# A decoder trunk's second feed-forward layer: two of four column slices of the down projection by seven block products

## The chip, the cores and the metric

The kernel runs on one core of a Trainium2 chip. The metric is the device time of one execution in microseconds (us); of several executions the median counts. Engines are named as in the profile: PE is TensorE (matmuls), PEld its weight loads, DVE is VectorE, ACT is ScalarE, POOL is GpSimd, SP is SyncE, which here only starts the transfers of weights.

## The reference

Two residual layers run over 256 tokens of width 2048, all in float32. The first mixes tokens with a convolution module, the second with a state-space module and a gated linear unit. Each is followed by a dense feed-forward layer of width 8192:

```python
def mlp(h, w_up, w_down):
    a = jax.nn.relu(h @ w_up)
    return (a * a) @ w_down
...
        h = rms_norm(x, mlp_norm[i])
        x = x + mlp(h, mlp_w_up[i], mlp_w_down[i])
    return rms_norm(x, final_norm)
```

The change concerns the feed-forward layer of i = 1, which is the last big stage. Its two weight matrices hold 2048 x 8192 float32 values each, 64 MB apiece, and every value is read from memory once per execution.

## The kernel before

**Splitting.** A float32 product is made from three matmuls of a type that keeps fewer bits: each operand is split into `hi` (a rounded copy) and `lo` (the rest), and hi*hi, hi*lo and lo*hi are summed in PSUM. For the weights, `split` (line 110) makes both parts for one half of a loaded piece: ACT writes `hi` (line 118), DVE writes `lo` = raw - hi (line 125), 128 x 1024 values each. There are four `hi` and four `lo` buffers, so a half can be split only when PE is done with the half four places earlier.

**Steps.** The weights come in steps of 1 MB (`raw`, three buffers), each of two halves. `run_steps` walks over the halves in order: it starts the loads of up to three steps beyond the current one, issues the splits up to three halves beyond the current one, and then the matmuls of the current half (`consume`). So the order in which steps are appended to `self.steps` is the order of PE's work. The framework then orders the instructions of each engine by priority; splits carry a raised one.

**The feed-forward layer** (`mlp`) cuts the width 8192 into eight slices of 1024. `up(s)` appends eight steps: four column groups of 256 (q), each with two halves of the contraction (kc). One half of such a step is eight matmuls with 512 columns (line 199: weights `hi` against both parts of the activations) and eight with 256 (line 202: `lo`). After every second step `relu2` turns the accumulator into squared, scaled and split activations `rT`. `down(s)` appends eight more: four output column slices of 512 (n), each with two halves of the contraction. Here the activations are the stationary operand; one half is twelve matmuls of 512 columns (lines 222 to 224), for two blocks of contraction, two token blocks of 128 and three products. After each n the sum in PSUM is added to `x` (`add_x`, line 820, 128 x 1024). The order is up(0), then up(s), down(s-1) for s = 1 to 7, then down(7). One pass of up(s) and down(s-1), from here on a slice, has 16 steps or 32 halves, 16 of up and 16 of down.

**Queues.** SP issues all weight loads (line 92) in step order; a load waits for its buffer, that is for the last `lo` made from it. DVE executes in the order written: `lo`, the activations' sums, and `add_x`.

## Time and profile before

| what | value |
|---|---|
| median of 3 runs | 1987.49 us (1987.08 to 1987.63) |
| span of the profiled execution | 1985.8 us |
| PE busy, share of the span | 1966.9 us, 99% |
| DVE busy | 1401.3 us, 71% |
| ACT busy | 952.4 us, 48% |
| last feed-forward stage, 1290 to 1970 us: PE busy of 680 us | 680.00 us |
| the same stage: DVE, ACT busy | 405.08 us, 317.93 us |
| the same stage: busy share of the DMA engines | 0.60 |

The profiled execution spans 1985.8 us from its first to its last instruction, and the median of the timed runs lies 1.7 us above that. In the rows below, a time in the first column of a timeline is the start in us from the beginning of the span. In a table by windows, each engine is given with its busy us in that window and, in brackets, its instructions. In a group of instructions, `x32 | 33.9, 1061` means 32 instructions, 33.9 us busy in all, 1061 ns for one; behind the second bar stands the idle time of the engine ahead of them and what ended it. Matmuls overlap in the pipeline: one lasts 0.39 us by the profile, but the next starts sooner, so PE's pace is read from the distance of starts.

### The profile page before, as it was taken

The page shows a single profiled execution, that of the slowest core. Times are in us where ns is not written, and L with a number is a line of the kernel's source. Part 1 is how long each engine was busy: PE and PEld are TensorE (multiplying, and loading weights), DVE is VectorE, ACT ScalarE, POOL GpSimd, SP SyncE. Part 2 cuts the span into 40 slices and gives each one's busy share as a digit, 9 for nine tenths or more (in the row PEclk, how much of TensorE's full clock was granted, in tenths as well). Part 3 has the DMA queues.
Part 4 walks back from the last instruction along what each step waited for, and adds up shares of the span by engine and source line. Part 5 has one row for each costly group of instructions (what it writes and reads, how often), then busy time and mean ns, then how long its engine had stood idle before and what let it go on. Part 6 is the DMA issues. An engine that isn't in the chain of part 4 may idle for free.

```text
span 1985.8 us, 28885 instructions
## 1 busy us (share of the span) xinstructions
PE 1966.9 (99%) x11604; PEld 1687.0 (85%) x11604; DVE 1401.3 (71%) x1904; ACT 952.4 (48%) x1179; POOL 274.8 (14%) x252
## 2 busy tenths in 40 slices
PE   8999999999999999999999999999999999999998
PEld 8999788888888888888888788888888888888887
DVE  6899798888787777777558847565555565555655
ACT  6443655544444544444445445454444454444444
POOL 3998300000000221222010000000000000000000
PEclk9999999999999999999999999999999999999999
DMA  8767458667686877877898865665666656565653
GB/s 228 190 184 207 147 183 267 206 226 245 200 260 192 214 229 253 265 246 238 319 308 298 304 215 186 191 191 189 193 190 192 190 191 191 190 213 190 192 191 128
DMA packets 317030, 428.49 MB, mean 216 GB/s; under 512 B 9761, under 2 KB 211553, under 8 KB 313537
## 3 DMA queue, kind: packets, MB, share of 16 engines
q1 hardware_dynamic: 300976, 384.59, 61.6%
q0 software_dynamic: 12352, 37.49, 6.3%
q10 hardware_dynamic: 3568, 4.56, 0.8%
q8 instruction: 91, 1.49, 0.3%
q14 instruction: 43, 0.35, 0.1%
HBM read 400.08 MB, written 34.91 MB: 219 GB/s over the span
## 4 chain that ended last, share of the span: by engine, by line
PE 96%; DVE 2%; DMA 1%; issue 0%; SPq 0%; POOL 0%; ACT 0%; POOLq 0%; DVEq 0%; ACTq 0%
PE acc L199 24%; PE acc L222 15%; PE acc L223 15%; PE acc L224 15%; PE acc L202 12%; PE acc L213 3%; PE acc L212 3%; PE acc L211 3%; PE pk L484 1%; DMA Vt<-Vd 0%; SPq L92 0%; PE kp L1113 0%; PE xw L1254 0%; DMA raw<-in_conv_w_in_dram 0%; PE xt L254 0%
## 5 line engine op out<-in xcount | busy, mean ns | idle before, releaser
L118 ACT ACTIVATE hi<-raw 128x1024 fp32r<-128x1024 f32 x672 | 711.6, 1060 | 953.5 <-PE acc L224 510.2
L125 DVE TENSOR_TENSOR lo<-raw,hi 128x1024 fp32r<-128x1024 f32 x611 | 747.9, 1226 | 505.6 <-ACT hi L118 501.3
L199 PE MATMUL acc<-hT,hi 128*128 128x512 f32 x2048 | 514.4, 393 | 0.0
L199 PEld LDWEIGHTS acc<-hT,hi 128*128 128x128 f32 x2048 | 368.9, 189 | 68.0 <-issue 1.6
L222 PE MATMUL acc<-hi,rT 128*128 128x512 f32 x992 | 387.2, 391 | 0.0
L223 PE MATMUL acc<-lo,rT 128*128 128x512 f32 x992 | 386.4, 390 | 0.0
L224 PE MATMUL acc<-hi,rT 128*128 128x512 f32 x992 | 386.0, 389 | 0.0
L202 PEld LDWEIGHTS acc<-hT,lo 128*128 128x128 f32 x2048 | 279.6, 190 | 20.0
L202 PE MATMUL acc<-hT,lo 128*128 128x256 f32 x2048 | 286.3, 282 | 0.0
L222 PEld LDWEIGHTS acc<-hi,rT 128*128 128x128 f32 x992 | 186.3, 188 | 39.6 <-issue 1.6
L224 PEld LDWEIGHTS acc<-hi,rT 128*128 128x128 f32 x992 | 186.3, 188 | 39.1
L223 PEld LDWEIGHTS acc<-lo,rT 128*128 128x128 f32 x992 | 186.3, 188 | 38.0 <-issue 0.2
L125 POOL TENSOR_TENSOR lo<-raw,hi 128x1024 fp32r<-128x1024 f32 x60 | 143.1, 2402 | 31.3 <-ACT hi L118 24.8
L211 PE MATMUL acc<-hT,hi 128*128 128x256 f32 x512 | 146.1, 286 | 0.9 <-ACT hi L118 0.9
L212 PE MATMUL acc<-hT,hi 128*128 128x256 f32 x512 | 145.7, 286 | 0.3 <-DVE hT L259 0.3
L213 PE MATMUL acc<-hT,lo 128*128 128x256 f32 x512 | 145.5, 286 | 0.0
L829 DVE SCALAR_TENSOR_TENSOR cv<-vT,dw,cv 128x256 f32<-128x256 f32 x348 | 141.3, 486 | 2.2 <-ACT cv L527 1.7
L820 DVE TENSOR_TENSOR x<-x,acc 128x1024 f32<-128x1024 f32 (+1 forms) x72 | 83.6, 1161 | 27.6 <-PE acc L224 22.0
L211 PEld LDWEIGHTS acc<-hT,hi 128*128 128x128 f32 x512 | 98.9, 193 | 3.0 <-issue 1.6
L222 PE MATMUL acc<-hi,yT 128*128 128x512 f32 x256 | 101.1, 395 | 0.0
L212 PEld LDWEIGHTS acc<-hT,hi 128*128 128x128 f32 x512 | 98.8, 193 | 2.2 <-issue 1.6
L223 PE MATMUL acc<-lo,yT 128*128 128x512 f32 x256 | 99.9, 390 | 0.6 <-DVE lo L125 0.6
(285 smaller groups left out, 1722.9 us busy)
## 6 DMA issues: line engine op xcount, KB each, us to landing
raw<-in_mlp_w_up_dram SPq DMA_DIRECT2D x128, 1024.0 KB, 5.8
raw<-in_mlp_w_down_dram SPq DMA_DIRECT2D x128, 1024.0 KB, 5.2
raw<-in_ssm_w_glu_dram SPq DMA_DIRECT2D x32, 1024.0 KB, 5.5
raw<-in_conv_w_in_dram SPq DMA_DIRECT2D x60, 512.0 KB, 5.6
raw<-in_conv_w_out_dram SPq DMA_DIRECT2D x16, 1024.0 KB, 5.2
Vd<-bv POOLq DMA_DIRECT2D x16, 512.0 KB, 6.3
Md<-Kd POOLq DMA_DIRECT2D x32, 256.0 KB, 7.2
Wt<-Wd SPq DMA_DIRECT2D x8, 1024.0 KB, 10.1
```

Of the source, the lines that this page charges most:

```text
L118: self.nc.scalar.activation(hi, sl, AF.Copy)
L125: ins = eng.tensor_tensor(out=lo, in0=sl, in1=hi.bitcast(F32), op=ALU.subtract)
L199: mm(accs[m], lhsT=hi[:, kk, cs[m]], rhs=xT(k0 + kk), start=first and kk == 0, stop=False)
L202: mm(accs[m][:, 0:T], lhsT=lo[:, kk, cs[m]], rhs=xT(k0 + kk)[:, 0, :], start=False, stop=last and kk == 3)
L211: mm(accs[m], lhsT=hi[:, kk, c], rhs=x[:, 0, :], start=first and kk == 0, stop=False)
L212: mm(accs[m], lhsT=hi[:, kk, c], rhs=x[:, 1, :], start=False, stop=False)
L213: mm(accs[m], lhsT=lo[:, kk, c], rhs=x[:, 0, :], start=False, stop=last and kk == 3)
L222: mm(acc[:, b, :], lhsT=ak[:, 0, t], rhs=hi[:, kk, :], start=first and kk == 0, stop=False)
L223: mm(acc[:, b, :], lhsT=ak[:, 0, t], rhs=lo[:, kk, :], start=False, stop=False)
L224: self.mm_last = mm(acc[:, b, :], lhsT=ak[:, 1, t], rhs=hi[:, kk, :], start=False, stop=last and kk == 1)
L820: return self.nc.vector.tensor_tensor(out=out, in0=a, in1=b, op=op)
L829: return self.nc.vector.scalar_tensor_tensor(out=out, in0=a, scalar=s, in1=b, op0=op0, op1=op1)
```

## The change

In the second layer, for slices 0 to 6, the output columns n = 0 and 1 of the down projection are computed by a scheme of seven block products in place of eight. The output is taken as 2 x 2 blocks C (two token blocks of 128 by two column slices of 512), the activations as 2 x 2 blocks A (token block by the parity of the 128-wide contraction block), and the weights as 2 x 2 blocks B (parity by column slice; a block is 512 x 512 values, 1 MB). With

S1 = A22 - A21, S2 = -S1 - A11, S3 = A11 - A21, S4 = -S2 - A12,

three PSUM banks take the products: p = A11*B11, then + S2*(B11+B12+B22), then + S3*(B12+B22), then + A22*(B11+B12+B22+B21); q = A12*B21; r = S1*(B11+B12), then + S4*B22. After each product the bank's current content is added to or subtracted from one 128 x 512 block of `x` (`takes`). The columns n = 2 and 3 and slice 7 keep the earlier scheme.

What the code does for it: `relu2_forms` takes the place of `relu2` and makes eight forms per contraction block (A21, A11, A22, A12, S1 to S4), so that `rT` of a slice is two tiles of the old size. `add_chain` adds a step whose weights are summed: the first block of a chain (X or Y) is loaded into a `sum` tile of the new pool `wide`, and each later one into `raw` and then added to the sum by DVE (line 941) when its half is due for splitting. One step (the second load of B12, for Y) has no matmuls. `raw` tiles are now half as large, six instead of three, in the whole program, and every load is issued as two. The tiles with the tag `t4` move into a pool that is closed before `wide` is opened. For these slices, up(s) and down(s-1) are no longer one behind the other but mixed step by step, in the order u0 m0 u1 m1 u2 m2 u3 d0 u4 m3 m4 u5 m5 u6 d1 m6 u7 m7 (u: a step of up; m: a step of the seven products, m3 the one without matmuls; d0 and d1: the two steps each of n = 2 and n = 3).

On PE, where a slice of the second layer goes from its up steps to its down steps, there stood (lines 199 and 202 up, 222 to 224 down):

```order
L199 MATMUL acc<-hT,hi 128x512 x8
L202 MATMUL acc<-hT,lo 128x256 x8
L199 MATMUL acc<-hT,hi 128x512 x8
L202 MATMUL acc<-hT,lo 128x256 x8
L222 MATMUL acc<-hi,rT 128x512
L223 MATMUL acc<-lo,rT 128x512
L224 MATMUL acc<-hi,rT 128x512
```

Now, around u4 and m4 of a slice (lines 228 and 231 are the up matmuls, 723 to 725 those of a product, `mp` the bank p), and so on through the slice:

```order
L228 MATMUL acc<-hT,hi 128x512 x8
L231 MATMUL acc<-hT,lo 128x256 x8
L228 MATMUL acc<-hT,hi 128x512 x8
L231 MATMUL acc<-hT,lo 128x256 x8
L723 MATMUL mp<-hi,rT 128x512
L724 MATMUL mp<-lo,rT 128x512
L725 MATMUL mp<-hi,rT 128x512
L723 MATMUL mp<-hi,rT 128x512
L724 MATMUL mp<-lo,rT 128x512
L725 MATMUL mp<-hi,rT 128x512
```

Where 32 groups of eight up matmuls ran and then 64 triples of down matmuls in a row, a product of twelve matmuls now stands between two up steps.

On DVE, the same place in an up step before (line 808 to 810 and 238 are `relu2`):

```order
L125 TENSOR_TENSOR lo<-raw,hi 128x1024 x3
L808 TENSOR_TENSOR t<-acc,t 128x512
L810 SCALAR_TENSOR_TENSOR t<-t,bcs 128x256 x2
L125 TENSOR_TENSOR lo<-raw,hi 128x1024
L238 TENSOR_TENSOR rT<-u,rT 128x2x256
L125 TENSOR_TENSOR lo<-raw,hi 128x1024 x2
L820 TENSOR_TENSOR x<-x,acc 128x2x512
```

Now, from the splits of u6 to those of m6 (152 makes `lo`, 927, 928 and 267 belong to `relu2_forms`, 941 is any plain sum, 950 a difference with a sign; `v` holds S1 to S4):

```order
L941 TENSOR_TENSOR sum<-sum,raw 128x1024
L941 TENSOR_TENSOR v<-u 128x128 x2
L152 TENSOR_TENSOR lo<-raw,hi 128x1024
L267 TENSOR_TENSOR rT<-u,rT 128x512
L152 TENSOR_TENSOR lo<-raw,hi 128x1024
L950 SCALAR_TENSOR_TENSOR v<-v,u 128x128
L941 TENSOR_TENSOR sum<-sum,raw 128x1024 x2
L950 SCALAR_TENSOR_TENSOR v<-v,u 128x128
L152 TENSOR_TENSOR lo<-sum,hi 128x1024 x2
L267 TENSOR_TENSOR rT<-v,rT 128x512
```

The sums of the weights for m6 and m7 now stand in DVE's queue ahead of m6's `lo` parts, and each of them waits for a load.

On SP, loads of a slice in the middle of the layer, before and then now:

```order
L92 DMA raw<-in_mlp_w_up_dram 128x8x256 x8
L92 DMA raw<-in_mlp_w_down_dram 128x4x512 x8
```

```order
L101 DMA raw<-in_mlp_w_up_dram 128x4x256 x2
L101 DMA sum<-in_mlp_w_down_dram 128x2x512 x2
L101 DMA raw<-in_mlp_w_down_dram 128x2x512 x2
L101 DMA raw<-in_mlp_w_up_dram 128x4x256 x2
L101 DMA raw<-in_mlp_w_down_dram 128x2x512 x2
L101 DMA raw<-in_mlp_w_up_dram 128x4x256 x2
L101 DMA raw<-in_mlp_w_down_dram 128x2x512 x6
```

A slice issued 16 loads of 1 MB and now issues 40 of 0.5 MB.

```diff
@@ -48,6 +49,10 @@
...
+        self.t4_guard = tc.tile_pool(name="quad", bufs=4)
+        self.quad = self.t4_guard.__enter__()
+        self.wide = None
...
-        return self.tmp.tile(shape, F32, tag="t4", name=name)
+        return self.quad.tile(shape, F32, tag="t4", name=name)
...
+    def add_chain(self, view, chain, consume=None):
+
+        self.steps.append((view, chain, consume, "x"))
...
@@ -92,28 +101,46 @@
...
-        if not half:
-            self.raws[i] = self.w.tile(shape, F32, tag="raw", name="raw", bufs=3)
-        raw = self.raws[i]
+        self.loaded = i + 1
+        chain = None
+        if pre == "x":
+            chain, shape = shape, [P, 4, 512]
+            if self.wide is None:
+                self.t4_guard.__exit__(None, None, None)
+                self.wide = self.ctx.enter_context(self.tc.tile_pool(name="wide", bufs=4))
         nk = shape[1] // 2
-        k = slice(0, shape[1]) if half is None else slice(half * nk, half * nk + nk)
-        if len(shape) == 4:
-            for j in range(shape[2]):
-                self.fetch(raw[:, k, j, :], view[:, k, j, :])
-        else:
-            self.fetch(raw[:, k], view[:, k])
-        self.loaded = i + 1
+        for hf in (0, 1) if half is None else (half,):
+            k = slice(hf * nk, hf * nk + nk)
+            size = [P, nk] + list(shape[2:])
+            if chain is not None:
+                if hf in chain:
+                    raw = self.raws[2 * i + hf] = self.w.tile(size, F32, tag="raw", name="raw", bufs=6)
+                else:
+                    raw = chain[hf] = self.wide.tile(size, F32, tag="wd", name="sum")
+            else:
+                raw = self.raws[2 * i + hf] = self.w.tile(size, F32, tag="raw", name="raw", bufs=6)
+            if len(shape) == 4:
+                for j in range(shape[2]):
+                    self.fetch(raw[:, :, j, :], view[:, k, j, :])
+            else:
+                self.fetch(raw, view[:, k])
...
-        raw = self.raws[i] if half == 0 else self.raws.pop(i)
-        nk = raw.shape[1] // 2
-        sl = raw[:, half * nk:(half + 1) * nk]
-        hi = self.w.tile([P, nk] + list(raw.shape[2:]), F32R, tag="hi", name="hi", bufs=4)
-        lo = self.w.tile([P, nk] + list(raw.shape[2:]), F32R, tag="lo", name="lo", bufs=4)
+        _, chain, consume, pre = self.steps[i]
+        if consume is None:
+            return None
+        if pre == "x":
+            sl = chain[half]
+            if h in self.raws:
+                self.tt(sl, sl, self.raws.pop(h), ALU.add)
+        else:
+            sl = self.raws.pop(h)
+        hi = self.w.tile(list(sl.shape), F32R, tag="hi", name="hi", bufs=4)
+        lo = self.w.tile(list(sl.shape), F32R, tag="lo", name="lo", bufs=4)
...
-            if half == 0 and pre is not None:
+            if half == 0 and callable(pre):
                 pre()
+            if consume is None:
+                continue
...
@@ -687,36 +716,100 @@
...
-        def up(s):
+        def products(acc, s, i, hi, lo, half, first):
+            mm = partial(self.nc.tensor.matmul, acc, skip_group_check=True)
+            for jj in range(2):
+                F = rT[s][half][:, jj]
+                mm(lhsT=F[:, 0, i, :], rhs=hi[:, jj, :], start=first and half == jj == 0, stop=False)
+                mm(lhsT=F[:, 0, i, :], rhs=lo[:, jj, :], start=False, stop=False)
+                self.mm_last = mm(lhsT=F[:, 1, i, :], rhs=hi[:, jj, :], start=False, stop=half == jj == 1)
+
+        def seven(s, n):
+
+
+            v = w_dn[s * 1024:(s + 1) * 1024].rearrange("(k two p) c -> two p k c", two=2, p=P)
+            B = lambda r, c: v[r, :, :, (n + c) * 512:(n + c + 1) * 512]
+            x = self.x
+            c11, c12, c21, c22 = (x[:, b, (n + c) * 512:(n + c + 1) * 512] for b in range(2) for c in range(2))
...
+            acc = {}
+
+            def part(form, bank, first, *takes):
+                def consume(hi, lo, half):
+                    if first and half == 0:
+                        acc[bank] = self.bank([P, 512], name="m" + bank)
+                    products(acc[bank], s, form, hi, lo, half, first)
+                    if half == 1:
+                        with self.tc.high_priority(offset=URGENT):
+                            for c, op in takes:
+                                self.tt(c, c, acc[bank], op)
+                return consume
+            A11, A22, A12, S1, S2, S3, S4 = range(1, 8)
+            add, sub = ALU.add, ALU.subtract
+            X, Y = {}, {}
+            load = self.add_chain
+            plain = lambda b, c: self.add(b, [P, 4, 512], c)
+            return [lambda: load(B(0, 0), X, part(A11, "p", True, (c11, add))),
+                    lambda: plain(B(1, 0), part(A12, "q", True, (c11, add))),
+                    lambda: load(B(0, 1), X, part(S1, "r", True, (c22, sub))),
+                    lambda: load(B(0, 1), Y),
+                    lambda: load(B(1, 1), X, part(S2, "p", False, (c12, sub))),
+                    lambda: plain(B(1, 1), part(S4, "r", False, (c12, sub))),
+                    lambda: load(B(1, 1), Y, part(S3, "p", False, (c22, sub))),
+                    lambda: load(B(1, 0), X, part(A22, "p", False, (c21, add)))]
...
-                            if q == 0:
+                            if formed(s):
+                                if q % 2 == 0:
+                                    rT.setdefault(s, []).append(self.blk_tile([P, 2, 2, 8, P], F32R, name="rT"))
+                            elif q == 0:
                                 rT[s] = self.blk_tile([P, 8, 2, T], F32R, name="rT")
-                            rT["acc"] = self.acc2()
-                        A = rT["acc"]
+                            rT["uacc"] = self.acc2()
+                        A = rT["uacc"]
...
+                            if formed(s):
+                                act = lambda: self.relu2_forms(A, rT[s][q // 2][:, q % 2])
+                            else:
+                                act = lambda: self.relu2(A, rT[s], 2 * q)
...
-        def down(s):
+        def down(s, only=None):
             for n in range(NS):
+                if only not in (None, n):
+                    continue
...
-                        self.mm_t(rT["acc"], lambda kk: rT[s][:, k0 + kk], hi, lo,
-                                  kc == 0 and half == 0, kc == 1 and half == 1)
+                        acc = rT["acc"]
+                        if not formed(s):
+                            self.mm_t(acc, lambda kk: rT[s][:, k0 + kk], hi, lo,
+                                      kc == 0 and half == 0, kc == 1 and half == 1)
+                        else:
+                            for kk in range(2):
+                                for b in range(NB):
+                                    F = rT[s][kc][:, half, :, 2 * kk + 1 - b, :]
+                                    for i, (f, w) in enumerate(((0, hi), (0, lo), (1, hi))):
+                                        self.mm_last = self.nc.tensor.matmul(
+                                            acc[:, b, :], lhsT=F[:, f, :], rhs=w[:, kk, :],
+                                            start=kc == half == kk == i == 0, stop=kc == half == kk == 1 and i == 2)
...
@@ -765,10 +858,18 @@
...
+        formed = lambda s: layer == 1 and s < nsl - 1
         up(0)
         for s in range(1, nsl):
-            up(s)
-            down(s - 1)
+            if not formed(s - 1):
+                up(s)
+                down(s - 1)
+                continue
+            m = seven(s - 1, 0)
+            u = [partial(up, s, k) for k in range(8)]
+            d = [partial(down, s - 1, n) for n in (2, 3)]
+            for e in (u[0], m[0], u[1], m[1], u[2], m[2], u[3], d[0], u[4], m[3], m[4], u[5], m[5], u[6], d[1], m[6], u[7], m[7]):
+                e()
         down(nsl - 1)
...
@@ -815,6 +916,26 @@
...
+    def relu2_forms(self, acc, R):
+
+        nc = self.nc
+        t = self.t2([P, 2, T], name="t")
+        u = self.t2([P, 4, P], name="u")
+        v = self.t2([P, 4, P], name="v")
+        nc.scalar.activation(t, acc[:, :, T:2 * T], AF.Copy)
+        nc.vector.tensor_tensor(out=t, in0=acc[:, :, 0:T], in1=t, op=ALU.add)
+        nc.vector.scalar_tensor_tensor(out=t, in0=t, scalar=0.0, in1=self.rstdB.broadcast_to([P, 2, T]),
+                                       op0=ALU.max, op1=ALU.mult)
+        nc.scalar.activation(u.rearrange("p (m b) t -> p m b t", m=2)[:, :, ::-1, :],
+                             t.rearrange("p m (b t) -> p m b t", b=2), AF.Square)
+        a21, a11, a22, a12 = (u[:, i, :] for i in range(4))
+        self.tt(v[:, 0, :], a22, a21, ALU.subtract)
+        self.stt(v[:, 1, :], v[:, 0, :], -1.0, a11, ALU.mult, ALU.subtract)
+        self.tt(v[:, 2, :], a11, a21, ALU.subtract)
+        self.stt(v[:, 3, :], v[:, 1, :], -1.0, a12, ALU.mult, ALU.subtract)
+        self.hsplit(u, R[:, 0, 0:4, :], R[:, 1, 0:4, :])
+        self.hsplit(v, R[:, 0, 4:8, :], R[:, 1, 4:8, :])
```

12 lines of the change are left out of this document (9 added, 3 removed).

## The prediction

> **What bounds the kernel now.** I read the page's shares first, then the chain of waits, then a table by windows for the stage that is changed.
>
> ```profile
> span 1985.8 us, 28885 instructions
> ...
> PE 1966.9 (99%) x11604; PEld 1687.0 (85%) x11604; DVE 1401.3 (71%) x1904; ACT 952.4 (48%) x1179; POOL 274.8 (14%) x252
> ...
> PE 96%; DVE 2%; DMA 1%; issue 0%; SPq 0%; POOL 0%; ACT 0%; POOLq 0%; DVEq 0%; ACTq 0%
> ```
>
> ```profile
> core 0: us, PE busy (x) PEld busy (x) DVE busy (x) ACT busy (x) POOL busy (x), PEclk, DMA share, GB/s
> 100.00:320.00 220.00, 218.76 (x1621) 192.20 (x1621) 204.28 (x464) 112.86 (x158) 113.22 (x61) 1.00 0.66 194
> 320.00:1000.00 680.00, 680.00 (x3706) 577.07 (x3705) 517.77 (x622) 321.32 (x385) 86.48 (x128) 1.00 0.76 239
> 1378.20:1466.40 88.20, 88.20 (x450) 75.38 (x449) 51.84 (x52) 40.55 (x45) 0.00 (x0) 1.00 0.61 190
> 1466.40:1554.60 88.20, 88.20 (x450) 75.36 (x449) 51.83 (x52) 40.55 (x45) 0.00 (x0) 1.00 0.61 191
> ```
>
> The two windows of 88.20 us are one slice of the second feed-forward layer each: PE is never idle, its granted clock is full, DVE works 51.8 us and ACT 40.6, the DMA engines 0.61 of the time. Here only PE's work sets the time. What PE's work costs is read from the distance of starts:
>
> ```profile
> 1501.35 2.00 PE L199 MATMUL acc<-hT,hi 128*128 128x512 f32 x8
> ...
> 1504.14 2.00 PE L199 MATMUL acc<-hT,hi 128*128 128x512 f32 x8
> ...
> 1505.99 1.11 PE L202 MATMUL acc<-hT,lo 128*128 128x256 f32 x8
> ...
> 1507.28 1.22 DVE L125 TENSOR_TENSOR lo<-raw,hi 128x1024 fp32r<-128x1024 f32 x1 [0.17 <-ACT hi L118]
> ...
> 1543.81 0.39 PE L222 MATMUL acc<-hi,rT 128*128 128x512 f32 x1
> ...
> 1546.53 0.39 PE L222 MATMUL acc<-hi,rT 128*128 128x512 f32 x1
> ```
>
> An up half lasts 1504.14 - 1501.35 = 2.79 us; twelve down matmuls last 1546.53 - 1543.81 = 2.72 us, 0.227 each. 16 x 2.79 + 16 x 2.72 = 88.2, the slice.
>
> **The change, part by part.**
>
> *PE.* Columns n = 0 and 1 took four down steps of 24 matmuls, 96. Seven products of 12 are 84. So 12 x 0.227 = 2.72 us less per slice, and over seven slices **19.0 us**. That holds if matmuls that all add to one bank keep their distance, six in a row here and twelve there:
>
> ```profile
> 1966.70 0.39 PE L232 MATMUL acc<-hi,rT 128*128 128x512 f32 x1
> ...
> 1967.84 0.39 PE L234 MATMUL acc<-hi,rT 128*128 128x512 f32 x1
> ```
>
> These are the first and the last of six into one bank: 1.14 / 5 = 0.228. The slice on PE becomes 85.5 us, if nothing makes PE wait.
>
> *DVE.* The prices, from one slice:
>
> ```profile
> L125 DVE TENSOR_TENSOR lo<-raw,hi 128x1024 fp32r<-128x1024 f32 x33 | 40.4, 1225 | 35.2 <-ACT hi L118 35.2
> L820 DVE TENSOR_TENSOR x<-x,acc 128x1024 f32<-128x1024 f32 x4 | 4.9, 1222 | 1.6 <-PE acc L224 1.6
> L810 DVE SCALAR_TENSOR_TENSOR t<-t,bcs 128x256 f32<-128x256 f32 x8 | 3.0, 422 | 0.1
> L238 DVE TENSOR_TENSOR rT<-u,rT 128x512 fp32r<-128x512 f32 x4 | 2.8, 692 | 0.0
> L808 DVE TENSOR_TENSOR t<-acc,t 128x512 f32<-128x512 f32 x4 | 2.7, 684 | 0.0
> ```
>
> Splits: 32 halves become 38 (16 up, 14 products, 8 of n = 2 and 3): 38 x 1.225 = 46.6. Sums of weights: 8 x 1.22 = 9.8 (same size as the row of line 820). Takes from the banks: 7 of 128x512 at 0.68 = 4.8; the whole adds that remain: 2 x 1.22 = 2.4. Activations, four times: 0.684, one 128x512 in place of two 128x256 (at most 0.84), two splits at 0.692, and four sums of 128x128, whose nearest rows are
>
> ```profile
> L820 DVE TENSOR_TENSOR pt<-pv 128x128 f32<-128x128 f32 x14 | 5.8, 412 | 0.1
> ...
> L820 DVE TENSOR_TENSOR rt<-R 128x128 f32<-128x128 f32 x2 | 0.6, 310 | 0.0
> ```
>
> I take 0.40 (bounds 0.31 and 0.42): 4.5 each, 18.0. The sum is **81.6 us** per slice (80.2 to 82.0) against 51.8 before and against PE's 85.5: DVE is 95% full, with 3.9 us to spare. That such a load need not stop PE shows in 100 to 320 us, where DVE worked 204.28 of 220 us (93%) and PE 218.76.
>
> An average is not enough, since DVE takes its queue in order, so I keep a ledger by stretches of PE (a u step 5.6 us, an m step 2.7, d0 or d1 10.9), with the work of DVE in the order it will have: u0 m0: 4 `lo` 4.9, activations of the last u7 4.5, one take 0.7, 10.1 against 8.3, behind by 1.8. u1 m1, with the sums for m2: 8.0 against 8.3, 1.5. u2 m2 with activations: 10.1, behind by 3.3, the most. u3 d0: 11.7 against 16.5, caught up. u4 m4 with activations 10.1: 1.8; u5 m5 with the sums for m6: 1.5; u6 d1 m6: 18.6 against 19.2, 0.9; u7 m7: 5.6 against 8.3, none. What lag is free: a `lo` starts as soon as PE leaves the half four places earlier (the row at 1507.28 follows the end at 1507.10), and is wanted three halves later. For a product's half these are two up halves and one product half, 2 x 2.79 + 1.36 = 6.9; less the `hi` before it, 1.06 on ACT, and its own 1.23, plus 0.23 for the matmul with `hi` alone, 4.9 us are free. The worst lag is 3.3: **no stall of PE**. Without that cover each us of lag beyond 4.9 costs 7 us.
>
> *ACT*, from the same slice:
>
> ```profile
> L118 ACT ACTIVATE hi<-raw 128x1024 fp32r<-128x1024 f32 x32 | 33.9, 1061 | 47.5 <-PE acc L224 25.8 <-PE acc L199 21.7
> L237 ACT ACTIVATE rT<-u 128x512 fp32r<-128x512 f32 x4 | 2.5, 634 | 0.1
> ```
>
> Six more `hi` (6.4) and four more splits of activations (2.5): 40.6 + 8.9 = 49.5 of 85.5. It hides behind PE.
>
> *DMA and SP.* A slice loads 20 MB where it loaded 16, in 85.5 us: the share becomes 0.61 x 20/16 x 88.2/85.5 = 0.79; 320 to 1000 us ran at 0.76 with PE full. SP issues 40 loads for 16, and one takes
>
> ```profile
> 1140.12 0.37 SPq L92
> ...
> raw<-in_mlp_w_down_dram SPq DMA_DIRECT2D x64, 1024.0 KB, 5.1
> raw<-in_mlp_w_up_dram SPq DMA_DIRECT2D x57, 1024.0 KB, 5.8
> ...
> raw<-in_conv_w_in_dram SPq DMA_DIRECT2D x28, 512.0 KB, 5.6
> ...
> bb<-in_ssm_b_re_dram POOLq DMA_DIRECT2D x1, 512.0 KB, 3.5
> ```
>
> 16 x 0.37 = 6 us before, 40 x 0.37 = 15 us now, of 85.5. How long a 0.5 MB piece of these weights takes to land the trace does not show: 3.5 us (the same size on another queue) to 5.6 (the same size with shorter rows); I take 4.7, near the whole piece's 5.1. It matters at one place, u6 d1 m6. DVE's sums for m7 stand there in its queue ahead of m6's `lo`, and the second sum's load can be issued only when the second half of d1's second step is split. Counting from the end of u6's first half: that `lo` is done at 2.79 + 0.17 + 1.23 + some queue, 5.1; the load lands at 5.1 + 4.7 = 9.8; sum, one small sum and m6's `lo` follow, 12.65; PE wants it after u6's second half, four halves of d1 and one matmul, 2.79 + 10.88 + 0.23 = 13.9. Slack 1.2; it is gone at a landing of 5.95 us. The other six sums have more work of PE between.
>
> *Halved loads in the rest of the program.* PE is idle 1985.8 - 1966.9 = 18.9 us, mostly at the start, the end and in the state-space stage. Smaller pieces may move that by 1.5 us either way; I take none.
>
> *Sum.* 1985.8 - 19.0 + 1.4 (0.2 us per slice for small misses in the ledger) = 1968.2 us of span; the median lies 1.7 above the span: **1969.9 us**.
>
> The Trainium skill (Perfetto Trace Analysis, section Matmuls) asks that independent matmul groups rotate through different PSUM banks, so that one group's evacuation overlaps the next group's matmuls. Bank p goes against it: four products, three of which begin only when DVE has taken the content before. By the rule the three takes of 0.68 us would stand open, 3 x 0.68 x 7 = 14 us. By the order now, at least one up step of 5.6 us stands between two uses of p, which is why I add nothing.
>
> **The rivals.**
>
> *A late load stalls PE at m6* (gain smaller). For it: the share of DMA rises to 0.79. Against: the bounds of 3.5 to 5.6 us lie below 5.95. Each us above costs 7 us; a landing of 7.5 us gives 1969.9 + 10.9 = 1980.8 us.
>
> *DVE sets the pace* (slower). Place: its queue in products with sums. The eight sums per slice wait for loads that are issued only after DVE itself has freed a buffer, and nothing behind them can pass. For it: 3.9 us of slack is all DVE has, where it idled 36 us before. Against: the ledger, and the 93% row. It decides from 3.9 us of such waits per slice; the gain is gone at 3.9 + 2.7 = 6.6. With 1.4 us per sum, 11.2 in all, a slice takes 85.5 + 7.3 = 92.8, 4.6 more than before, 32 us in all: 2020 us. That engine queues are strict FIFO is what the Trainium skill says of VectorE too (TensorE: Matmul & The Clock Gate, section Architectural detail); no row here tests it.
>
> *The saving is eaten at bank p* (no change): if takes come late behind two `lo`, the three uses stay open, 3 x 0.68 x 7 = 14 us: 1984 us. Against: 5.6 us between them.
>
> **How the numbers follow.** Likeliest, PE stays the bound: 0.66, with a range of its own of 1967 to 1973. Late loads 0.17 (1973 to 1985), DVE 0.12, bank p 0.05. A measurement of this kernel tells 0.2%, 4 us, from no change: faster means below 1983.5. So faster 0.80, same 0.08, slower 0.12. The range 1967 to 1983 leaves out the slower rival, the open bank, and the ends of the rest, 2 in 10.
>
> **What would show it.** Right: in a window of the layer a slice repeats every 85.5 to 86 us with PE busy throughout; DVE is busy 80 to 82 us of it, mostly waiting for nothing longer than 1 us; line 941's sums show little idle time before them that ends with a DMA; starts of lines 723 to 725 are 0.227 apart. Wrong: PE idle before lines 723 or 724, released by DVE's `lo` (DVE's pace) or, behind it, by a load; sums of 128x1024 dearer than 1.22; matmuls of bank p released by DVE's takes.

## The result and the profile after

| | before | after |
|---|---|---|
| median | 1987.56 us (1987.08 to 1987.67, four runs) | 1967.25 us (1967.18 to 1967.40, four runs) |
| ratio, with its 95% interval | | 0.9896 (0.9882 to 0.9910) |
| span of the profiled execution | 1985.8 us | 1965.5 us |

The changed kernel is 1.0% faster: 20.3 us, by the medians as by the two spans. The page of the changed kernel, with the span, the busy times and the chain of work that ended last:

```profile
span 1965.5 us, 30158 instructions
...
PE 1947.3 (99%) x11520; PEld 1670.6 (85%) x11520; DVE 1547.6 (79%) x2149; ACT 1008.5 (51%) x1249; POOL 275.8 (14%) x252
...
PE 97%; DVE 1%; DMA 1%; issue 0%; POOL 0%; ACT 0%; SPq 0%; POOLq 0%; DVEq 0%; ACTq 0%
```

There are 84 matmuls fewer (11520 for 11604: seven slices of twelve), PE's busy time is 19.6 us less, and PE still is nearly the whole chain. The table by windows of the changed kernel, one stretch ahead of the layer and one slice of it (columns as in the prediction's table: PE, PEld, DVE, ACT, POOL, PEclk, DMA share, GB/s):

```profile
1140.00:1160.00 20.00, 20.00 (x149) 16.46 (x148) 8.09 (x8) 8.42 (x10) 0.00 (x0) 1.00 0.75 263
...
1461.00:1546.50 85.50, 85.50 (x438) 73.12 (x438) 73.42 (x89) 48.32 (x54) 0.00 (x0) 1.00 0.75 246
```

A slice is 85.50 us long, where it was 88.20, and PE is busy in all of it at full clock. DVE works 73 us of the slice. In the layer, from 1290 us on, the list of PE's waits is empty.

**Where the 20.3 us lie.** A matmul that both kernels have just ahead of the layer (the one that spreads the row scales, `bc`) serves as a mark. In the timeline of the kernel before, this mark and a product of the state-space stage:

```profile
1150.69 1.94 PE L1346 MATMUL mv<-Vt,SS 128*32 128x128 f32 x56 [0.64 <-DMA Vt<-Vd]
...
1281.66 0.59 PE L296 MATMUL bc<-dg,ones 128*128 128x256 f32 x2
```

The same two in the changed kernel:

```profile
1149.23 1.98 PE L1467 MATMUL mv<-Vt,SS 128*32 128x128 f32 x64
...
1280.25 0.59 PE L325 MATMUL bc<-dg,ones 128*128 128x256 f32 x2
...
1957.41 0.28 PE L263 MATMUL acc<-hi,rT 128*128 128x256 f32 x1
```

The mark comes 1.41 us earlier, so that much was gained before the changed layer began. One piece of it can be seen: the product waited 0.64 us for a transfer, and no longer does. From the mark to the end it is 704.14 us before and 685.25 now, 18.89 less; the matmuls account for 7 x 2.72 = 19.04. The last row is the program's last matmul. From the mark to it are 677.16 us, and 696.16 before (the row stands with the first experiment): 19.00 less. Nothing else is left to explain.

**DVE after.** Groups of DVE's instructions in that slice (count, busy us and mean ns of one, idle time ahead of them):

```profile
L152 DVE TENSOR_TENSOR lo<-raw,hi 128x1024 fp32r<-128x1024 f32 x28 | 33.9, 1220 | 8.0 <-ACT hi L145 8.0
...
L941 DVE TENSOR_TENSOR sum<-sum,raw 128x1024 f32<-128x1024 f32 x9 | 11.0, 1222 | 5.5 <-DMA raw<-in_mlp_w_down_dram 5.3
...
L941 DVE TENSOR_TENSOR v<-u 128x128 f32<-128x128 f32 x8 | 1.9, 283 | 0.0
```

The large operations cost per piece what the prediction said (1.22 us), the small ones 0.28 and not 0.40. In this window nine sums wait 5.5 us for loads; over the seven slices DVE's sums wait 26.7 us, 3.8 per slice. How far apart DVE's operations start shows in its timeline (start, duration, instruction; in brackets the idle time before it):

```profile
1461.96 1.22 DVE L152 TENSOR_TENSOR lo<-raw,hi 128x1024 fp32r<-128x1024 f32 x1
1463.10 0.68 DVE L941 TENSOR_TENSOR x<-x,mr 128x512 f32<-128x512 f32 x1
1463.70 1.22 DVE L152 TENSOR_TENSOR lo<-raw,hi 128x1024 fp32r<-128x1024 f32 x1
...
1472.18 1.23 DVE L941 TENSOR_TENSOR sum<-sum,raw 128x1024 f32<-128x1024 f32 x1 [0.90 <-DMA raw<-in_mlp_w_down_dram]
...
1473.53 2.35 DVE L152 TENSOR_TENSOR lo<-sum,hi 128x1024 fp32r<-128x1024 f32 x2
```

An operation of 1.22 us is followed by the next after 1.14 us, one of 0.68 after 0.60: consecutive operations overlap by some 0.085 us. Those that wait for something do not. In this window the durations of all of DVE's groups add up to 79.9 us and DVE is busy 73.4, so the overlap is worth some 6 us of the difference between the 81.6 us reckoned and the 73 measured. The rest is prices that were too high, the small sums above all (16 x 0.12 = 1.9 us). The last two rows are the tight place, a late sum ahead of m6's `lo`. The product that needs it, and the next use of bank p, in PE's timeline:

```profile
1475.13 0.39 PE L723 MATMUL mp<-hi,rT 128*128 128x512 f32 x1
1475.36 0.39 PE L724 MATMUL mp<-lo,rT 128*128 128x512 f32 x1
...
1483.41 0.40 PE L723 MATMUL mp<-hi,rT 128*128 128x512 f32 x1
```

The first `lo` of m6 is done at about 1473.53 + 1.22 = 1474.75 and used at 1475.36: 0.6 us to spare. By the same reading the seven slices have from 0.4 us (ready at 1902.42, used at 1902.85) to 1.7 us (1559.19 and 1560.85), with 1.2 in the middle. m6's twelve matmuls end at 1475.13 + 12 x 0.227 = 1477.85, and m7 begins in bank p 5.6 us later. The transfers of the layer, from the part on DMA issues over 1375 to 1890 us (KB each, median us from issue to landing), and behind them the two loads for m7 in the shown slice, issued from 1464.94 us on:

```profile
raw<-in_mlp_w_down_dram SPq DMA_DIRECT2D x120, 512.0 KB, 5.3
...
DMA to landing us min/median/max: 5.1/5.6/6.1
```

The 6.1 us are those of the second load, for which the late sum at 1472.18 waits. In the seven slices this load takes 5.3 to 6.1 us.

### The profile page after: what moved, and what is told of

Same layout as the page of the kernel before. It is cut to its first block, busy times and chain, and to the rows that moved or that the text cites. A ratio compares the mean times of both kernels' runs of the same rounds, so it can differ in the third digit from the quotient of the medians.

```text
span 1965.5 us, 30158 instructions
## 1 busy us (share of the span) xinstructions
PE 1947.3 (99%) x11520; PEld 1670.6 (85%) x11520; DVE 1547.6 (79%) x2149; ACT 1008.5 (51%) x1249; POOL 275.8 (14%) x252
## 4 chain that ended last, share of the span: by engine, by line
PE 97%; DVE 1%; DMA 1%; issue 0%; POOL 0%; ACT 0%; SPq 0%; POOLq 0%; DVEq 0%; ACTq 0%
PE acc L228 24%; PE acc L231 12%; PE acc L251 11%; PE acc L252 10%; PE acc L253 10%; PE acc L810 8%; PE acc L240 3%; PE acc L242 3%; PE acc L241 3%; PE mp L723 1%; PE mp L724 1%; PE mp L725 1%; PE pk L513 1%; PE mr L723 1%; PE mr L724 1%; PE mr L725 1%
## 5 line engine op out<-in xcount | busy, mean ns | idle before, releaser
L145 ACT ACTIVATE hi<-raw 128x1024 fp32r<-128x1024 f32 x644 | 681.6, 1060 | 780.4 <-PE acc L253 332.8
L152 DVE TENSOR_TENSOR lo<-raw,hi 128x1024 fp32r<-128x1024 f32 x583 | 710.7, 1222 | 314.4 <-ACT hi L145 312.1
L228 PEld LDWEIGHTS acc<-hT,hi 128*128 128x128 f32 x2048 | 371.9, 189 | 70.7 <-issue 1.6
L251 PE MATMUL acc<-hi,rT 128*128 128x512 f32 x544 | 212.9, 392 | 0.0
L252 PE MATMUL acc<-lo,rT 128*128 128x512 f32 x544 | 212.1, 390 | 0.0
L253 PE MATMUL acc<-hi,rT 128*128 128x512 f32 x544 | 211.7, 389 | 0.0
L810 PE MATMUL acc<-hi,rT 128*128 128x512 f32 x448 | 140.4, 389 | 0.0
L251 PEld LDWEIGHTS acc<-hi,rT 128*128 128x128 f32 x544 | 102.1, 188 | 22.4 <-issue 1.6
L253 PEld LDWEIGHTS acc<-hi,rT 128*128 128x128 f32 x544 | 102.1, 188 | 21.5
L252 PEld LDWEIGHTS acc<-lo,rT 128*128 128x128 f32 x544 | 102.2, 188 | 20.9 <-issue 0.2
L145 ACT ACTIVATE hi<-sum 128x1024 fp32r<-128x1024 f32 x70 | 74.4, 1062 | 72.4 <-PE acc L810 41.4
L240 PEld LDWEIGHTS acc<-hT,hi 128*128 128x128 f32 x512 | 98.8, 193 | 3.4 <-issue 2.1
```

The source lines that it names most:

```text
L145: self.nc.scalar.activation(hi, sl, AF.Copy)
L152: ins = eng.tensor_tensor(out=lo, in0=sl, in1=hi.bitcast(F32), op=ALU.subtract)
L228: mm(accs[m], lhsT=hi[:, kk, cs[m]], rhs=xT(k0 + kk), start=first and kk == 0, stop=False)
L240: mm(accs[m], lhsT=hi[:, kk, c], rhs=x[:, 0, :], start=first and kk == 0, stop=False)
L251: mm(acc[:, b, :], lhsT=ak[:, 0, t], rhs=hi[:, kk, :], start=first and kk == 0, stop=False)
L252: mm(acc[:, b, :], lhsT=ak[:, 0, t], rhs=lo[:, kk, :], start=False, stop=False)
```

## The experiments

All compute the whole of the reference. Each is compared with the kernel before on the same chip, by ratio; the changed kernel's 0.9896 is the figure to hold them against. The theory under test: PE's own work is the time of the layer, DVE is hidden because it has room to spare and because the products are spread between up steps. The rivals: DVE is nearly full, and the place u6 d1 m6 or bank p is about to stop PE.

### Each part alone

**Halved loads without the products**: the kernel before, with `raw` in halves.

```diff
-            self.raws[i] = self.w.tile(shape, F32, tag="raw", name="raw", bufs=3)
+            raw = self.raws[2 * i + hf] = self.w.tile([P, nk] + list(shape[2:]), F32, tag="raw", name="raw", bufs=6)
```

> The kernel before with one part of the change alone: every load is issued as two halves into six raw tiles of half the size; no block products, no mixed order. The changed kernel gained 20.3 us, of which 19.0 are matmuls; 1.3 us are left over. Theory A (the left-over is that of the halved loads, which land earlier in the state-space stage, where PE stood idle 0.6 us more before): 1986.2 to 1986.6 us, with PE busy 20.0 of 20 us around 1140 to 1160 us. Theory B (it comes with the new order or with the products): 1987.5 us, as before.

Measured: 1986.72 us, ratio 0.9997 (0.9987 to 1.0006), which the times cannot tell from no change. The profiled span is 1984.9, 0.9 below that of the kernel before, and the records show what it is made of. The mark and one of the last matmuls, in its timeline:

```profile
1279.97 0.59 PE L293 MATMUL bc<-dg,ones 128*128 128x256 f32 x2
...
1976.13 0.28 PE L231 MATMUL acc<-hi,rT 128*128 128x256 f32 x1
```

The mark is 1.7 us earlier than before (1281.66). From the last matmul, which is the lower row, to the end it is 8.8 us; before, it was 1985.8 - 1977.82 = 8.0, from

```profile
1977.82 0.28 PE L234 MATMUL acc<-hi,rT 128*128 128x256 f32 x1
```

From the mark to the last matmul it is 696.16 us in both. So in these traces the halved loads give some 1.4 to 1.7 us ahead of the layer and nothing in it, and this run lost 0.8 of them again in the closing norm, for which no cause was looked for. The mark stands between 1279.7 and 1280.4 us in eleven of the twelve traces with six halved `raw` tiles and at 1281.4 in the twelfth, that of the last experiment below. Only one trace has whole loads, so the size of this gain is not secured.

**The mixed order without the products**: halved loads, all eight forms made, but n = 0 and 1 by the earlier scheme with 96 matmuls.

```diff
+            m = [partial(down, s - 1, n, kc) for n in (0, 1) for kc in range(2)]
+            for e in (u[0], u[1], m[0], m[1], u[2], u[3], m[2], m[3], u[4], u[5], d[0], u[6], u[7], d[1]):
```

> The changed kernel without the products: the eight forms of the activations, the halved loads and an order that mixes up and down steps stay (here two up steps, then one column slice of down), but all four column slices are computed in the earlier way. Theory A (only fewer matmuls save time): 1967.25 + 19.0 = 1986.3 us, a slice of 88.2 us. Theory B (the mixing or the halved loads save several us): 1975 to 1983 us.

Measured: 1986.71 us, ratio 0.9996 (0.9987 to 1.0006): no change, as in the run above. From the mark to the last matmul (1280.13 to 1976.29 us) it is again 696.16 us, so mixing the steps and making the forms gains and costs nothing by itself.

**The scheme in four slices of the seven.**

```diff
-        formed = lambda s: layer == 1 and s < nsl - 1
+        formed = lambda s: layer == 1 and s < 4
```

> The changed kernel with the seven products in slices 0 to 3 only; slices 4 to 6 are computed as before the change. Theory A (each slice gives back its twelve matmuls, 2.72 us, and nothing else): 1967.25 + 3 x 2.72 = 1975.4 us, with a period of 85.5 us in the first four slices and of 88.2 in the others. Theory B (part of the gain comes once, with the first slice or with the start or end of the stage): nearer to 1967 or to 1979 us.

Measured: 1975.86 us, ratio 0.9941 (0.9926 to 0.9956). Its span, 1973.4, is 7.9 us above the 1965.5 of seven slices; three slices of 2.72 are 8.2. From the mark to the last matmul (1280.03 to 1965.32 us) it is 685.29 us for 677.16, 8.13 more, 2.71 per slice. The gain goes with the number of slices. Together these three runs show that the gain inside the layer is the removed matmuls alone.

### How much room DVE has

In every up step of the changed slices the `lo` of the first half (eight per slice), or of both halves (sixteen), is made twice, the second time as the first.

```diff
             with self.behind(self.lo_gate) if self.lo_gate is not None else nullcontext():
                 ins = eng.tensor_tensor(out=lo, in0=sl, in1=hi.bitcast(F32), op=ALU.subtract)
+                if h in self.twice:
+                    ins = eng.tensor_tensor(out=lo, in0=sl, in1=hi.bitcast(F32), op=ALU.subtract)
...
+                    if layer == 1 and s > 0:
+                        self.twice.update(2 * len(self.steps) + k for k in (0,))
```

(With sixteen, the last line runs over (0, 1).)

> The changed kernel, in which DVE writes the lo part of the first half of each up step twice, in slices 1 to 7 of the second layer: eight more instructions of 128x1024 per slice, same output. Theory A (a DVE instruction behind another costs the distance of starts, 1.14 us; DVE needs 73 us per slice and has 12 to spare): 73 + 9.1 = 82 of 85.5, the time stays at 1967 to 1969 us. Theory B (it costs the profile's 1.22 us; DVE stands at 81.6 us as the prediction reckoned): 81.6 + 9.8 = 91.4, 5.9 us per slice over PE, 1967 + 41 = 2008 us.

> The changed kernel with the lo part of both halves of each up step written twice in slices 1 to 7 (16 more DVE instructions per slice, twice the dose of the run with eight). With eight, DVE was busy 82 us per slice and the time rose by 4 us. Theory A (DVE costs the distance of starts): 73 + 16 x 1.14 = 91.2 us per slice against PE's 85.5, so DVE sets the pace: 5.7 us or a little more per slice over seven slices, 1967 + 40 = 2005 to 2015 us. Theory B (what cost 4 us was the later lo of single halves, not DVE's sum): twice the 4 us, 1975 us.

Measured: with eight 1971.51 us, ratio 0.9920 (0.9906 to 0.9935); with sixteen 2011.79, ratio 1.0127 (1.0110 to 1.0144). One window of the layer with eight:

```profile
1547.00:1633.00 86.00, 85.92 (x438) 73.21 (x437) 82.16 (x97) 48.58 (x54) 0.00 (x0) 1.00 0.74 246
```

Its list of PE's waits in the layer (us in total, times, longest):

```profile
PE acc L234 <- DVE lo L155: 3.1, 3, 1.6
```

The same window with sixteen:

```profile
1547.00:1633.00 86.00, 81.86 (x412) 68.04 (x412) 85.63 (x98) 45.15 (x50) 0.00 (x0) 1.00 0.68 224
```

and the first of its waits from 1375 to 1890 us:

```profile
PE acc L234 <- DVE lo L155: 13.4, 8, 2.4
```

Nine us more of DVE per slice (8 x 1.14) cost 4.2 us of span in the whole kernel. That is not the nothing that the first theory expected: three times a `lo` came late, although the sum over the slice fits. Had there been 3.9 us of room, 5.2 us of each slice would have been open, 36 us in all. Eighteen us more fill DVE (85.63 of 86): 73 + 16 x 1.14 = 91.2 us of work against 85.5, 40 us in seven slices, and 43 were measured by the spans (2008.2 for 1965.5). So DVE's room is about 12 us per slice, as the distance of starts gives it, and past that DVE sets the pace.

### What the spread is worth

**The same steps, with the products behind the up steps** as the two stood before.

```diff
-            for e in (u[0], m[0], u[1], m[1], u[2], m[2], u[3], d[0], u[4], m[3], m[4], u[5], m[5], u[6], d[1], m[6], u[7], m[7]):
+            for e in u + m + d:
```

> The changed kernel with the order of steps undone: in each slice all eight up steps, then the seven products in a row, then n = 2 and n = 3. Same work on every engine. Theory A (the spread is what hides DVE and the loads): the products last 19.0 us on PE but need 14 lo, 8 sums and 7 takes on DVE, 22 x 1.14 + 7 x 0.60 = 29 us; less some 5 us of work ahead, PE waits 4 to 8 us per slice, 1995 to 2025 us, slower than before. Theory B (only the sums over a slice count, DVE 73 of 85.5 us): 1967 us.

Measured: 2047.74 us, ratio 1.0305 (1.0288 to 1.0322), and the granted clock is 0.986. One slice, and in it the stretch of the products, in the table by windows:

```profile
1484.00:1581.00 97.00, 89.44 (x441) 74.88 (x440) 74.85 (x89) 48.95 (x54) 0.00 (x0) 0.96 0.67 217
1560.00:1581.00 21.00, 13.44 (x47) 9.70 (x46) 21.00 (x26) 10.89 (x11) 0.00 (x0) 0.83 0.55 185
```

A slice takes 97 us. While the products run, DVE is busy 21.00 of 21 us, although over the slice it has hardly more to do than in the changed kernel (74.85 for 73.42). PE's timeline there:

```profile
1566.25 0.80 PE L724 MATMUL mp<-lo,rT 128*128 128x512 f32 x1 [3.96 <-DVE lo L152]
...
1567.27 0.63 PE L723 MATMUL mp<-hi,rT 128*128 128x512 f32 x1
1567.70 0.63 PE L724 MATMUL mp<-lo,rT 128*128 128x512 f32 x1
...
1570.65 0.39 PE L724 MATMUL mp<-lo,rT 128*128 128x512 f32 x1
...
1573.40 0.39 PE L725 MATMUL mr<-hi,rT 128*128 128x512 f32 x1
1574.77 0.47 PE L723 MATMUL mp<-hi,rT 128*128 128x512 f32 x1 [0.97 <-DVE x L941]
```

and DVE's take that this last row waits for:

```profile
1573.92 0.70 DVE L941 TENSOR_TENSOR x<-x,mp 128x512 f32<-128x512 f32 x1
```

Three things are to be seen. PE waits 3.96 us for a `lo`. After that the starts are 0.43 us apart and not 0.23, until 1570.65, that is for some four us: the wait cost time a second time, in clock. The Trainium skill (TensorE: Matmul & The Clock Gate, Part 1) says that an idle window of about 3.4 us halves PE's clock and that a busy one of that length restores it; the 3.96 us of idle time and the 0.43 in place of 0.23 agree. And the last row is bank p not yet free: PE has done with its product before in this bank at 1570.88 and has worked since on eleven matmuls in bank r, but DVE, with other work ahead in its queue, takes the content only at 1573.92, and PE waits 0.97 us. The sum fits: PE is not busy for 97 - 89.44 = 7.6 us, and busy 3.9 longer than 85.5, 11.5 us per slice in all. So the spread is worth 80 us here: the mean load of DVE is the same, only its place differs. The expectation of 4 to 8 us per slice holds for the waits; the whole was missed because the slower clock was not in the reckoning.

**m6 and m7 with no up step between them.**

```diff
-            for e in (..., u[6], d[1], m[6], u[7], m[7]):
+            for e in (..., u[6], d[1], u[7], m[6], m[7]):
```

> The changed kernel with the last up step of a slice moved ahead of m6, so that the two products m6 and m7, both in bank p, follow each other with only DVE's take between. Theory A (a take stands open where nothing lies between): PE waits at m7 for DVE's queue and the take of 0.68 us, 0.8 to 2 us per slice, 1973 to 1981 us. Theory B (the take costs PE nothing): 1967 us.

Measured: 1968.86 us, ratio 0.9905 (0.9890 to 0.9919), not to be told from the changed kernel by the times. The order in which the framework put PE's work was not the one meant: it moved m7 behind 24 of the 32 up matmuls of the next slice's first step. The last matmul of m6 and the first of m7 in PE's timeline:

```profile
1483.14 0.39 PE L725 MATMUL mp<-hi,rT 128*128 128x512 f32 x1
...
1488.05 0.39 PE L723 MATMUL mp<-hi,rT 128*128 128x512 f32 x1
```

There are 4.7 us of other work between the two products, and no matmul of a product waits for a take. So this is no test of adjacent products, and what a take costs with nothing between stays open. The run before it has the only price: 0.97 us, and there 2.5 us of other matmuls did not cover the take, because DVE came to it late. So the cover depends on DVE's queue and not on PE's work alone. The Trainium skill (Perfetto Trace Analysis, section Matmuls) asks for rotation through the banks; in the changed kernel going without it costs nothing.

### The tight place

**Five `raw` tiles in place of six**, so that loads start later.

```diff
-name="raw", bufs=6)
+name="raw", bufs=5)
```

> The changed kernel with five raw tiles of half a step in place of six, so that each load is issued one half later. Theory A (the tight place of the prediction: m6's lo stands behind the weight sums for m7, whose load waits for a raw tile; 0.6 us were to spare there): each load comes 1.4 to 2.8 us later, so PE waits 1 to 2 us per slice at m6, released by DVE's lo, 1974 to 1982 us. Theory B (loads have slack everywhere): 1967 us.

Measured: 1971.39 us, ratio 0.9918 (0.9904 to 0.9933). The loss does not lie in the changed layer. The second entry in its list of PE's waits over the whole span is one in the state-space stage:

```profile
PE mv L1467 <- DMA Vt<-Vd: 2.2, 2, 1.9
```

The mark in its timeline:

```profile
1284.15 0.59 PE L325 MATMUL bc<-dg,ones 128*128 128x256 f32 x2
```

The mark is 3.9 us later than in the changed kernel, and so is the end (1969.4 for 1965.5); the waits in the row above account for 2.2 of them. Within the layer PE is busy throughout, and no stall at m6 appears. The framework also put DVE's sums and PE's products in another order, so a later load at m6 was not cleanly tried.

**m6's first `lo` made three times**, two operations more per slice, and as a control the same at m1, where the prediction saw no tight place.

```diff
-                ins = eng.tensor_tensor(out=lo, in0=sl, in1=hi.bitcast(F32), op=ALU.subtract)
+                for _ in range(3 if h in self.thrice else 1):
+                    ins = eng.tensor_tensor(out=lo, in0=sl, in1=hi.bitcast(F32), op=ALU.subtract)
...
+                if e is m[6]:
+                    self.thrice.add(2 * len(self.steps))
```

> The changed kernel with the lo part of m6's first half written three times (2.3 us more of DVE per slice, at the place that the prediction called tight; in the changed kernel this lo was ready 0.6 us before PE took it). Theory A (that place is tight): PE waits 2.3 - 0.6 = 1.7 us per slice ahead of bank p's second matmul, 1967 + 12 = 1979 us. Theory B (DVE's 12 us of idle time per slice absorb it): 1967 us.

> The same dose at another place: the lo part of m1's first half written three times, which in the changed kernel was ready 4.6 us before PE took it. Both theories of the run with m6: no wait, 1967 us. Were DVE's sum over the slice what counts, this run and the one with m6 would come out alike.

Measured: at m6 1972.86 us, ratio 0.9927 (0.9912 to 0.9942); at m1 1970.47, ratio 0.9916 (0.9901 to 0.9930). PE's waits in the layer with m6:

```profile
PE acc L233 <- DVE lo L154: 4.1, 6, 1.0
```

one of them in its timeline, between the first and the second matmul of m6:

```profile
1476.02 0.39 PE L725 MATMUL mp<-hi,rT 128*128 128x512 f32 x1
...
1478.45 1.22 PE L233 MATMUL acc<-hT,lo 128*128 128x256 f32 x8 [0.23 <-DVE lo L154]
...
1481.35 0.39 PE L726 MATMUL mp<-lo,rT 128*128 128x512 f32 x1
```

and the waits with m1:

```profile
PE acc L233 <- DVE lo L154: 1.8, 6, 0.3
```

The 2.3 us of delay cost 5.3 us of span at m6 and 3.2 at m1, in seven slices 0.8 and 0.5 each. What waits is not the product but the up matmuls with the `lo` queued behind it. The reason is that the framework changed PE's order in both runs: it left only the first matmul of the dosed product in its place and put the other eleven behind 24 up matmuls, as the rows at 1476.02 and 1481.35 show for m6. So neither run measures the room at its place in the changed kernel, and how tight m6 is stays untested; neither expectation was met. The two intervals overlap; the difference rests on the spans and the waits.

### A second engine for the sums

**The eight sums per slice on GpSimd.**

```diff
-                self.tt(sl, sl, self.raws.pop(h), ALU.add)
+                self.nc.gpsimd.tensor_tensor(out=sl, in0=sl, in1=self.raws.pop(h), op=ALU.add)
```

> The changed kernel with the eight weight sums per slice on GpSimd, which is idle in this stage, in place of VectorE. Theory A (PE is the bound, DVE's share is hidden): DVE falls by about 9 us per slice, the time stays at 1967 us. Theory B (a sum on GpSimd takes 2.4 us, as its lo parts did in the first layer, and comes too late for the split that follows it): PE waits before products with sums, four of them per slice at up to 1 us, up to 28 us more.

Measured: 1971.79 us, ratio 0.9922 (0.9907 to 0.9937): no better than the changed kernel. DVE, relieved of 9 us of sums per slice, is busy longer and not shorter, 79.79 of 86 us, which neither theory expected:

```profile
1547.00:1633.00 86.00, 86.00 (x439) 73.25 (x438) 79.79 (x80) 48.26 (x55) 22.14 (x9) 1.00 0.75 245
```

Groups of this kernel from 1500 to 1700 us:

```profile
L152 DVE TENSOR_TENSOR lo<-raw,hi 128x1024 fp32r<-128x1024 f32 x66 | 89.8, 1374 | 13.1 <-ACT hi L145 13.0
L139 POOL TENSOR_TENSOR sum<-sum,raw 128x1024 f32<-128x1024 f32 x19 | 51.9, 2746 | 149.3 <-DMA raw<-in_mlp_w_down_dram 146.9 <-DVE v L950 2.4
...
L941 DVE TENSOR_TENSOR v<-u 128x128 f32<-128x128 f32 x20 | 18.2, 949 | 0.0
```

The small DVE sums went from 0.28 to 0.95 us. The timelines of POOL and DVE in this kernel show how, POOL's one row first:

```profile
1546.52 6.06 POOL L139 TENSOR_TENSOR sum<-sum,raw 128x1024 f32<-128x1024 f32 x2 [17.39 <-DMA raw<-in_mlp_w_down_dram]
...
1546.87 0.68 DVE L941 TENSOR_TENSOR x<-x,mr 128x512 f32<-128x512 f32 x1
1547.46 2.85 DVE L152 TENSOR_TENSOR lo<-raw,hi 128x1024 fp32r<-128x1024 f32 x1
1550.23 2.70 DVE L941 TENSOR_TENSOR v<-u 128x128 f32<-128x128 f32 x2
```

POOL works from 1546.52 to 1552.58, two sums of about 3 us. The DVE operation whose second input is in PSUM (`mr`) takes 0.68 as always. The two behind it, which read two tensors from SBUF, take 2.85 for 1.22 and 2.70 for 0.48, and the second ends 0.35 us after POOL. The Trainium skill (SBUF — State Buffer, section SBUF: two separate sides) says that a DVE operation with two SBUF inputs and a GpSimd operation that reads SBUF exclude each other for the whole instruction, and that DVE's own pair of ports waits on nobody; these rows agree in both.

**All four column slices by seven products, sums on GpSimd**, as far as the scheme goes.

```diff
-            m = seven(s - 1, 0)
+            a, b = seven(s - 1, 0), seven(s - 1, 2)
...
+            for e in (u[0], a[0], a[1], u[1], a[2], a[3], u[2], a[4], a[5], u[3], a[6], u[4], a[7], b[0], u[5], b[1], b[2], b[3], u[6], b[4], b[5], b[6], u[7], b[7]):
```

> The changed kernel with the scheme of seven products on all four column slices of slices 0 to 6, and the weight sums on GpSimd. PE has 12 matmuls less per slice again, 2.72 us, 82.8 us. DVE: 73 - 9 (sums gone) + 10 (six more lo, five more takes net) = 74 us. Loads: 24 MB per slice where it is 20 now. Theory A (PE stays the bound): 1967 - 19 = 1948 us. Theory B (the loads become the bound: 0.75 x 24/20 x 85.5/82.8 = 0.93 of the DMA engines, with loads issued only as tiles come free): PE waits several us per slice, 1960 to 2000 us.

Measured: 2103.68 us, ratio 1.0582 (1.0566 to 1.0597), clock 0.977. A window of the layer:

```profile
1547.00:1633.00 86.00, 72.94 (x331) 58.11 (x330) 82.81 (x72) 42.12 (x48) 43.21 (x14) 0.92 0.70 230
```

and two groups, the sums on POOL and the costliest of DVE, from 1500 to 1700 us:

```profile
L139 POOL TENSOR_TENSOR sum<-sum,raw 128x1024 f32<-128x1024 f32 x29 | 89.5, 3104 | 108.2 <-DVE lo L152 61.2 <-DMA raw<-in_mlp_w_down_dram 39.3 <-DVE v L949 7.7
L152 DVE TENSOR_TENSOR lo<-raw,hi 128x1024 fp32r<-128x1024 f32 x46 | 77.8, 1700 | 3.0 <-ACT hi L145 3.0
```

The share of DMA is 0.70, below that of the changed kernel, so it is not loads that hold the layer. The mean `lo` from `raw` has become 1.70 us and DVE is nearly full with fewer operations: the same exclusion, with twice the sums. But this order also puts two or three products in a row, which by itself cost 80 us above, and the clock is lower here too. How the loss divides among these was not tested. Neither expectation had them.

None of the twelve variants is faster than the changed kernel.

## Why the prediction was right, and where not

- **Time and sign.** 1969.9 us was forecast and 1967.25 measured, faster as forecast, at the very low end of the range of 1967 to 1983 (by the ratio, 0.9896 x 1987.56 = 1966.9, just below it). PE stayed the bound, which was the likeliest case. The mechanism was right; two terms of the sum were mis-sized, both the same way.
- **PE.** 19.0 us by twelve matmuls in seven slices: right. A slice measures 85.50, with PE busy throughout, and the stretch from the mark to the end became 18.89 shorter. That all twelve add to one bank did not change their distance (0.227).
- **The step that failed first: 1.4 us for "small misses in the ledger".** They measured nothing: no wait of PE in the layer, and 19.00 us less from the mark to the last matmul for the 19.0 reckoned. This was one half of the 2.7 us by which the span, 1965.5, came out below 1968.2.
- **The step that failed second: halved loads taken at nothing.** The mark comes 1.4 us earlier, within the bound of 1.5 stated, and with that the other half of the 2.7 is found. With halved loads alone it comes 1.7 us earlier, but against a single trace with whole loads, and by time this alone is below what a measurement tells.
- **DVE, 81.6 us with 3.9 to spare.** Mis-sized: 73 us, with 12 to spare. The prices of single operations were right, except for the small ones (0.28 for 0.40, some 2 us per slice); adding up durations was wrong by some 6, since the next operation starts 0.085 us before the one ahead ends in the records. The trace before had it already: the 1.22 us row of line 820 at 1548.77 was followed by a start at 1549.91. For PE the prediction read the distance of starts, for DVE it did not. The 1.4 us above was an allowance on a ledger with these prices, and the slower rival rested on the 3.9.
- **The slower rival.** DVE's sums were to set the pace from 3.9 us of waits for loads per slice. They wait 2.7 to 5.4 per slice, 3.8 in the mean, and PE does not notice: with 12 us to spare, 3.9 decides nothing. The mechanism is real, though: with sixteen `lo` more, DVE sets the pace at 2011.79 us.
- **The ledger by stretches.** Right in its result, no stall, with some luck: its prices were all too high, which errs on the safe side here. That a mean does not suffice was shown by the products in a row: the same work of DVE, and 80 us more.
- **A late load at m6.** 4.7 us was taken for the landing of 0.5 MB; it took 5.3 in the median, and at the place itself 5.3 to 6.1, once more than the 5.95 that was to decide. Yet 0.6 us were left in that slice. The limit was reckoned too low, again by adding durations: the load was issued 4.65 us after u6's first half (1466.08 and 1461.43 us), not 5.1, and what follows its landing took 2.6 us and not 2.85. The slack of 1.2 us lies in the middle of the measured 0.4 to 1.7, by two errors that cancel. How far a later load could go was not cleanly tried.
- **Bank p.** Right in its result: 5.6 us of other work stand between m6 and m7, and none of the matmuls waits for a take. But a take was priced at its own 0.68 us, and its place in DVE's queue counts as well: in the row of the products in a row it comes 2.6 us after the product's last matmul, and 0.97 us stay open.
- **ACT and DMA.** 49.5 us forecast and 48.3 measured; a share of 0.79 forecast and 0.75 measured. Neither bounds.

## What to carry to other kernels

Price every in-order engine by the distance of starts in its timeline, not by adding durations: the difference was some 6 us of an 85.5 us stage here, and with it how near to full the engine seemed. Where an engine off the bound gets more work, its place counts as much as its amount: the same DVE work between PE's long steps cost nothing, and in a row 80 us, a third of it because PE lost clock after its wait. Moving two-input work from DVE to GpSimd gave nothing back here, because the two take turns at it.

## What the runs showed of the hardware that was not expected

- DVE's records overlap: 1.22 us long and 1.14 apart (128 x 1024), 0.68 and 0.60 (128 x 512).
- After 3.96 us without work, matmuls started 0.43 us apart for some four us, and then 0.23 again.
- GpSimd's sums and DVE's operations with two SBUF inputs take turns: `lo` from `raw`, 1.22 us, became 1.37 in the mean with eight sums on GpSimd per slice and 1.70 with twice as many, and a sum on GpSimd itself went from 2.75 to 3.10 us. DVE operations with an input in PSUM were not slowed. The kernel before had such a row, unread at the time. In its first stage a DVE operation of 128 x 1024, a size that takes 1.22 us elsewhere, stands with 1.68 in the timeline, beside a GpSimd operation that began at 103.37 us and lasted 2.39:

```profile
105.17 1.68 DVE L569 TENSOR_TENSOR vT<-vT,shift 128x1024 f32<-128x1024 f32 x1
```
